# A hybrid decoder layer on one core: no written order of instructions, a timeline model that ranks them all, plain products for the first output pairs, and eight gate columns moved from w_out to the query projections

## The chip, the cores and the metric

The kernel runs on one core of a Trainium2 chip. A core has TensorE (PE; matrix products, with weight loads listed as PEld), VectorE (DVE), ScalarE (ACT), GpSimd (POOL) and SyncE (SP). Each engine works through its own queue of instructions in order and waits on semaphores for the others. Here SP's queue issues the loads of weights and inputs, POOL's queue issues the traffic with intermediate tensors in the chip's memory.

The metric is the device time of one execution, in microseconds (us), given as a median over runs.

## The reference

One decoder layer for 512 tokens of width D = 2048, in fp32. Cut to what matters:

```python
mod = silu(c) @ w_ada + b_ada                       # 6 x 2048 numbers
sh1, sc1, g1, sh2, sc2, g2 = split(mod, 6)
h = modulate(rms_norm(x, norm1_g), sh1, sc1)        # h * (1 + sc1) + sh1
u = h @ w_in                                        # conv, q and 3 x (k, v) columns, gates
y_conv = B * causal_depthwise_conv3(C * H)          # 1024 channels
y_attn = nsa_attention(q, ...)                      # 8 heads: compressed, selected, window
x = x + g1 * (concat([rms_norm(y_conv), rms_norm(y_attn)]) @ w_out)
h = modulate(rms_norm(x, norm2_g), sh2, sc2)
x = x + g2 * (square(relu(h @ w_ff1)) @ w_ff2)      # 8192 hidden columns
out = rms_norm(x, normf_g)
```

## The kernel before

**Arithmetic.** The products need more accuracy than one pass gives. Each operand is split into a high half (a rounded copy, made by ScalarE) and a low half (the difference, made by VectorE). `mm3` (L93 to L95) issues three matmuls for each pair of 128 x 128 blocks: high x high (L93), high x low (L94) and low x high (L95). So each weight blob of 128 x 1024 costs one ScalarE pass (`wh`, L83 or L800) and one VectorE pass (`wl`, L84 or L801) before its matmuls. Activations lie with channels on the partitions and tokens along the row.

**adaLN.** Each of the 96 columns of `mod` is a dot product of 2048 numbers with silu(c): two VectorE multiply-and-sum passes over a 128 x 1024 load of w_ada (`scr`, L134, followed by a short read of the sum), and one small instruction (L139) that adds both halves and the bias.

**The front** (from L98). Sums of squares of x give the row norm `rs` (L178), spread over the partitions as a 128 x 512 tile and copied to `rb`. Then 32 steps follow, each with one 128 x 1024 blob of `w_kv` or `w_cv` and one k of the 16 channel blocks: 24 matmuls of 512 columns into eight banks. Beside them VectorE computes the scale and shift column of each next k, multiplies x by `rb` (`tokens`, L260) and makes the low half of h (`low`, L267); what is left of time goes to further w_ada columns from a list `todo`. All of this stage is written with `pinned[0] = True`: `pin` (L67 to L69) then marks an instruction to stay in program order, and the program interleaves the work by hand, with a count of VectorE time (`clock`) against the steps' (`ready`).

**After the front** `pinned[0]` is False (L411), and the tile framework's scheduler, in its default ranking, decides the order on each engine. The projections follow: the convolution columns (`project`, `w_conv`), the compression of keys and values (`compress`), the value columns, then the query columns (`w_q`). At places in these loops `more_ada` takes columns from `todo`: 16 columns of the first gate, 32 of the second scale and shift, and 8 of the second gate (M_G2). Attention runs over 2 groups and 4 blocks of 128 queries. Between the blocks stand eight products of the convolution half with `w_oc` (`out_conv`, its banks named `pw`), which serve as filler for TensorE; behind the last block the attention row norm, `row_bcast` (L178 to L182), the scaling `ya` (L766) and the splits `mixa` (L89, L90) make the operands of the attention half.

**w_out.** The attention half is multiplied by eight `w_oa` blobs; in this loop `ada` also computes the last eight columns of the second gate through `raw_blob`. Then `kept` splits eight blobs of `w_oa2`, `late_out(0)` makes the low half of the tokens (256) of the other 1024 output channels, `late_out(1)` the high half.

**The feed-forward part.** Each of 32 pairs of w_ff1 is a 2 x 2 block product done with 7 products rather than 8 (Winograd's form of Strassen's scheme). The weights of a pair are four blobs A11, A21, A22, A12; `operands` makes the seven weight operands, with four sums or differences of 128 x 1024 on VectorE (`sub`, L875) and seven splits (`hilo`, L800 and L801). The token operands B1, U6, T5, B2, T7, B3, T4 stay in memory; `low_tokens` and `high_tokens` make them from the normed rows. A product is 24 matmuls of 256 columns into a bank `pf`. `ff1` combines the products, applies relu and square, makes the seven operands of the next stage (`gt`, `gb`) and stores them through POOL. In the second stage, 8 rounds f load the seven token operands (`tk<-g`) and run w_ff2 in the same way. `ahead` puts products B1 and B2 of the first three pairs ahead while `high_tokens` is computed.

The start of the feed-forward part before:

```python
    late_out(0)
    low_tokens()
    late_out(1)
    ahead(0, B1)
    row_norm(bankf, sacc, D, r2, 2, 4)
    ahead(1, B1)
    high_tokens(0)
    ...
    high_tokens(3)
    for p in range(32):
        ff1(p)
```

Of the kernel before, what the change touches and what calls it, by code (L numbers as in the profile page):

```python
# [15 lines left out]
P = 128  # L16
# [24 lines left out]
def hybrid_layer(ctx: ExitStack, tc: tile.TileContext, a, out):  # L41
# [56 lines left out]
    pinned[0] = True  # L98
# [43 lines left out]
    def ada(n, blob=None):  # L142
        acc = small.tile([P, 2], F32, name="acc")
        for i in range(2):
            if blob is None:
                w = slot(name="wa")[:, :1024]
                nc.sync.dma_start(out=w, in_=a["w_ada"][2 * n + i])
# [20 lines left out]
    def row_norm(bank, square, width, dst, t0=0, t1=NQ):  # L168
        total = bank()
        for t in range(t0, t1):  # L170
            nc.tensor.matmul(total[:, t:t + 1], square[:, t * P:(t + 1) * P], ones[:, 0:1],
                             start=True, stop=True)
        row_bcast(bank, total[:, t0:t1], width, dst[:, t0 * P:t1 * P])

    def row_bcast(bank, total, width, dst):
# [5 lines left out]
        if dst is not None:  # L181
            nc.scalar.activation(dst, ps[:, :n * P], AF.Copy)  # L182
# [64 lines left out]
    for i in range(4):  # L247
# [7 lines left out]
        + [M_G2 * NK + k for k in range(8)]  # L255
# [188 lines left out]
    nc.sync.dma_start(out=cw2, in_=a["vec"][:, V_END:])  # L444

    def compress(which, src):
# [3 lines left out]
        for hf in range(2):  # L450
            t = slot(name="ct")
            nc.vector.memset(t[:, 1024:SLOT], 0.0)
            tv = t[:, :1024].rearrange("p (l g n) -> p l g n", g=NG, n=32)
            n = 32 - hf
            for g in range(NG):
                nc.vector.tensor_tensor(
                    out=tv[:, :, g, :n],
                    in0=src[g].rearrange("p (n l) -> p l n", l=16)[:, :, hf:],
                    in1=pe[:, hf * 16:hf * 16 + 16, None].to_broadcast([P, 16, n]), op=OP.add)
            if hf:  # L460
                nc.vector.memset(tv[:, :, :, 31:], 0.0)
            hi = slot(F32R, name="chi")
            lo = slot(F32R, name="clo")
            nc.scalar.activation(hi, t, AF.Copy)
            nc.vector.tensor_tensor(out=lo, in0=t, in1=hi.bitcast(F32), op=OP.subtract)
# [18 lines left out]
        nc.scalar.activation(hid, pc[:64, :256], AF.Copy)  # L484
        nc.vector.tensor_tensor(out=tt, in0=hid, in1=hid, op=OP.mult)
        nc.vector.tensor_scalar(tt, tt, 0.044715, 1.0, op0=OP.mult, op1=OP.add)
        nc.vector.tensor_tensor(out=tt, in0=tt, in1=hid, op=OP.mult)
        nc.scalar.activation(tt, tt, AF.Tanh, scale=math.sqrt(2.0 / math.pi))
        nc.vector.tensor_scalar(tt, tt, 1.0, 0.5, op0=OP.add, op1=OP.mult)
        nc.vector.tensor_tensor(out=hid, in0=hid, in1=tt, op=OP.mult)  # L490
        pt = bank()
        for i in range(2):
            nc.tensor.transpose(pt[:, i * 64:i * 64 + 64], hid[:, i * P:(i + 1) * P], ident[:64, :64])
        hidt = temp([P, 2, NG, 32], name="hidt")
        nc.scalar.activation(hidt.rearrange("p i g n -> p (i g n)"), pt[:, :P], AF.Copy)
        yield
        if which == 0:
            pk = bank()
            for i in range(2):
                nc.tensor.matmul(pk[:, :64], w2[i], hidt[:, i].rearrange("p g n -> p (g n)"),  # L500
                                 start=i == 0, stop=i == 1)
            for g in range(NG):
                split(kslc[g][:, :, :32], pk[:, g * 32:g * 32 + 32])
        else:
            pad = temp([P, 2, NG, P], name="hpad")
            nc.vector.memset(pad, 0.0)
            nc.vector.tensor_copy(pad[:, :, :, :32], hidt)
            for g in range(NG):
                pv = bank()
                for i in range(2):  # L510
                    nc.tensor.matmul(pv[:, :P], pad[:, i, g], w2[i], start=i == 0, stop=i == 1)
# [7 lines left out]
    for j in range(8):  # L519
# [13 lines left out]
        if 3 * j >= 8:  # L533
            nc.scalar.activation(z, got[0], AF.Copy)
            got[0] = z
        nc.vector.tensor_tensor(out=v, in0=got[1], in1=got[0], op=OP.mult)
        nc.scalar.activation(z, v, AF.Identity, scale=cw[2], bias=vec[:, V_CB + j:V_CB + j + 1])
        for t, d in ((1, 1), (0, 2)):
            nc.vector.scalar_tensor_tensor(out=z[:, d:], in0=v[:, :T - d], scalar=cw[t], in1=z[:, d:],
                                           op0=OP.mult, op1=OP.add)  # L540
        nc.vector.tensor_tensor(out=y, in0=got[2], in1=z, op=OP.mult)
        if j == 0:
            sacc = accum()
            nc.scalar.activation(sacc, y, AF.Square)
        else:
            sq = temp(name="sq")
            nc.scalar.activation(sq, y, AF.Square)
            nc.vector.tensor_tensor(out=sacc, in0=sacc, in1=sq, op=OP.add)
# [7 lines left out]
    for g in range(NG):  # L556
# [13 lines left out]
        for t in range(NQ):  # L570
            if t % 2 == 0:
                vp = pair(F32R, name="vv").rearrange("p h (t c) -> p h t c", t=2)
            vv[g, t] = vp[:, :, t % 2]
            nc.scalar.activation(vv[g, t][:, 0], pv[t][:, :256], AF.Copy)
            nc.vector.tensor_tensor(out=vv[g, t][:, 1], in0=pv[t][:, :256],
                                    in1=vv[g, t][:, 0].bitcast(F32), op=OP.subtract)
            gt = gates[:, t, g].rearrange("p r b -> p (r b)")
            nc.scalar.activation(gt, pv[t][:, 256:268], AF.Tanh, scale=0.5)
            nc.vector.tensor_scalar(gt, gt, 1.0, 0.5, op0=OP.add, op1=OP.mult)
# [9 lines left out]
    def mixed(j):  # L589
        y = ys[j // 2][:, j % 2]  # L590
        nc.vector.scalar_tensor_tensor(out=y, in0=y, scalar=vec[:, V_GC + j:V_GC + j + 1], in1=rc,
                                       op0=OP.mult, op1=OP.mult)
# [13 lines left out]
    for g in range(NG):  # L606
# [9 lines left out]
        for n in range(NR):  # L616
# [3 lines left out]
            nc.scalar.activation(raws[-1], pq[n], AF.Copy)  # L620
# [20 lines left out]
    def out_conv(m):  # L641
# [8 lines left out]
        nc.vector.scalar_tensor_tensor(out=x1[m // 2][:, m % 2], in0=ps, scalar=col(M_G1, m),  # L650
                                       in1=out_conv.x[:, (m % 2) * T:(m % 2 + 1) * T],
                                       op0=OP.mult, op1=OP.add)

    def attention(g, qb):
# [4 lines left out]
        nc.vector.memset(pcx[:, NR:], 0.0)  # L659
        pc = pcx[:, :NR]  # L660
        cm = cmask[:, qb]
        for b in (1, 2):
# [7 lines left out]
            for r in range(NR):  # L670
                q = qs[g * NR + r]
                s = pss.tile([P, T], F32, name="s")
                nc.tensor.matmul(s[:, :w], q[:, 0, qc], kt[:, 0, c0:c0 + w], start=True, stop=False)
# [579 lines left out]
```

## Time and profile before

| what | value |
|---|---|
| median of 3 runs | 2223.15 us (2222.85 to 2224.5) |
| profiled execution | 2224.19 us |
| its span, first to last instruction | 2222.4 us |
| mean granted TensorE clock | 0.981 |
| TensorE busy, matmuls | 2131.6 us (96%), 14942 |
| VectorE busy, instructions | 1918.1 us (86%), 2998 |
| ScalarE busy | 1008.2 us (45%) |
| DMA | 453.61 MB, mean 204 GB/s |

The page counts the time in which an engine had at least one instruction in flight. Matmuls are pipelined and their ends are modelled, so that the spans of neighbours overlap: one of 256 columns is listed with 282 ns, though 427 of them start in 50 us. Idle time of TensorE is thus read better from the number of matmuls in a stretch than from the busy share. In a table of stretches each row has the stretch, its length, then for PE, PEld, DVE, ACT and POOL the busy time with the number of instructions in brackets, then the clock that was granted to TensorE (1.00 is full), the busy share of the DMA engines and the rate in GB/s. In a row of a group, "x176 | 211.0, 1220 | 8.1 <-DMA" reads: 176 instructions, 211.0 us busy, 1220 ns each, 8.1 us of idle time of that engine just before them, ended by a DMA. In a row of waits, "6.1, 1, 6.1" is the total, the number of times and the longest. In a timeline the first two numbers are the start and the duration in us.

The execution in stages, by that trace: the front up to 225, the projections up to about 575, attention up to about 793, w_out's attention half and `late_out` up to about 890, ff1 up to about 1575, ff2 to the end.

### The profile page before, as it was taken

To read this page: it belongs to the slowest core of one execution; us is meant where nothing else is said; L and a number is where in the kernel's file an instruction comes from. 1 tells how busy PE (TensorE), PEld (TensorE's weight loads), DVE (VectorE), ACT (ScalarE), POOL (GpSimd) and SP (SyncE) were. 2 spreads that over 40 slices of the span, in tenths; PEclk is the share of its full clock that TensorE was granted. 3 is DMA by queue.
4 is the path that set the end of the run, shared out by engine and by line. 5 is a ranking of instruction groups with operands and counts; after the bars stand their busy time and mean duration, and the time that the engine had idled before them with its cause. 6 is when DMAs were issued, how large, how long until landed. Compare 5 with 4: busy or idle time off the path is not lost.

```text
span 2222.4 us, 37637 instructions
## 1 busy us (share of the span) xinstructions
PE 2131.6 (96%) x14942; PEld 1969.9 (89%) x14942; DVE 1918.1 (86%) x2998; ACT 1008.2 (45%) x1468; POOL 193.6 (9%) x366
## 2 busy tenths in 40 slices
PE   6999989999999999799999999999899999999997
PEld 4777778898777779799999999999899999999996
DVE  8889978877496687999999999999799999999996
ACT  4431333222354435665666556666333333333353
POOL 0000000000000001021111111113211011011000
PEclk7999999999999999899999999999999999999998
DMA  8985686954211165276665666658865466366442
GB/s 343 336 323 180 237 313 256 356 216 180 86 39 57 57 266 185 81 233 209 199 196 195 199 211 196 201 190 283 296 241 195 157 237 233 119 237 235 151 146 95
DMA packets 143984, 453.61 MB, mean 204 GB/s; under 512 B 15809, under 2 KB 20161, under 8 KB 143809
## 3 DMA queue, kind: packets, MB, share of 16 engines
q1 hardware_dynamic: 91104, 322.22, 40.4%
q0 software_dynamic: 51616, 127.95, 17.2%
q8 instruction: 117, 1.92, 0.3%
q10 hardware_dynamic: 1088, 1.05, 0.1%
q14 instruction: 59, 0.48, 0.1%
HBM read 383.00 MB, written 68.16 MB: 203 GB/s over the span
## 4 chain that ended last, share of the span: by engine, by line
PE 75%; DVE 13%; ACT 5%; DMA 4%; issue 2%; SPq 0%; DVEq 0%; ACTq 0%; POOL 0%; POOLq 0%
PE pf L95 18%; PE pf L93 18%; PE pf L94 18%; PE ps L94 5%; PE ps L95 5%; PE ps L93 5%; DVE scr L134 3%; DVE wl L84 2%; DMA tk<-g 1%; DVE hl L801 1%; ACT wh L83 1%; PE pw L94 1%; PE pw L95 1%; PE pw L93 1%; PE pt L719 1%
## 5 line engine op out<-in xcount | busy, mean ns | idle before, releaser
L93 PE MATMUL pf<-tk,hl 128*128 128x256 f32 x3576 | 1008.0, 282 | 12.3 <-DMA tk<-g 6.0
L95 PE MATMUL pf<-tk,hl 128*128 128x256 f32 x3576 | 1005.5, 282 | 12.2 <-DVE hl L801 12.2
L94 PE MATMUL pf<-tk,hl 128*128 128x256 f32 x3576 | 1006.7, 282 | 1.3 <-DVE tk L872 1.3
L93 PEld LDWEIGHTS pf<-tk,hl 128*128 128x128 f32 x3576 | 678.2, 190 | 15.3 <-ACT hl L800 8.0
L95 PEld LDWEIGHTS pf<-tk,hl 128*128 128x128 f32 x3576 | 676.7, 190 | 14.8 <-DVE hl L801 14.7
L94 PEld LDWEIGHTS pf<-tk,hl 128*128 128x128 f32 x3576 | 677.0, 189 | 1.7 <-DVE tk L872 1.6
L800 ACT ACTIVATE hl<-rw 128x1024 fp32r<-128x1024 f32 x264 | 278.8, 1056 | 303.6 <-PE pf L95 254.9
L801 DVE TENSOR_TENSOR hl<-rw,hl 128x1024 fp32r<-128x1024 f32 x264 | 321.9, 1219 | 25.6 <-ACT hl L800 25.2
L800 ACT ACTIVATE hl<-sg 128x1024 fp32r<-128x1024 f32 x189 | 200.3, 1061 | 267.7 <-PE pf L95 242.9
L801 DVE TENSOR_TENSOR hl<-sg,hl 128x1024 fp32r<-128x1024 f32 x189 | 230.5, 1221 | 41.7 <-ACT hl L800 41.3
L134 DVE SCALAR_TENSOR_TENSOR scr<-wa,cs 128x1024 bf16<-128x1024 f32 x176 | 211.0, 1220 | 8.1 <-DMA wa<-in_w_ada 8.0
L83 ACT ACTIVATE wh<-raw 128x1024 fp32r<-128x1024 f32 (+1 forms) x105 | 110.8, 1059 | 221.0 <-PE ps L94 105.1
L84 DVE TENSOR_TENSOR wl<-raw,wh 128x1024 fp32r<-128x1024 f32 (+1 forms) x105 | 128.6, 1225 | 56.6 <-ACT wh L83 54.2
L875 DVE TENSOR_TENSOR sg<-sg,rw 128x1024 f32<-128x1024 f32 x126 | 153.5, 1219 | 0.9
L95 PE MATMUL ps<-h_m,wl 128*128 128x512 f32 x360 | 142.8, 397 | 2.5 <-DVE wl L84 2.4
L93 PE MATMUL ps<-h_m,wh 128*128 128x512 f32 x360 | 142.6, 396 | 2.4 <-ACT wh L83 1.2
L94 PE MATMUL ps<-h_m,wh 128*128 128x512 f32 x360 | 141.8, 394 | 0.0
L1049 DVE SCALAR_TENSOR_TENSOR x<-pf,mod,x 128x256 f32<-128x256 f32 x256 | 119.7, 479 | 17.9 <-PE pf L95 14.9
L93 PE MATMUL ps<-h,wh 128*128 128x512 f32 x280 | 113.2, 404 | 13.1 <-ACT wh L83 9.1
L95 PE MATMUL ps<-h,wl 128*128 128x512 f32 x280 | 113.7, 406 | 2.4 <-DVE wl L84 2.4
L94 PE MATMUL ps<-h,wh 128*128 128x512 f32 x280 | 113.3, 405 | 0.0
L1015 POOL DMA_DIRECT2D g<-gt x192 | 101.0, 532 | 86.4 <-DVE gt L872 81.2
(325 smaller groups left out, 2974.1 us busy)
## 6 DMA issues: line engine op xcount, KB each, us to landing
rw<-in_w_f SPq DMA_DIRECT2D x262, 512.0 KB, 4.3
wa<-in_w_ada SPq DMA_DIRECT2D x176, 512.0 KB, 6.2
tk<-g POOLq DMA_DIRECT2D x114, 512.0 KB, 8.1
g<-gt POOLq DMA_DIRECT2D x192, 256.0 KB, 5.0
raw<-in_w_conv SPq DMA_DIRECT2D x32, 512.0 KB, 6.6
raw<-in_w_kv SPq DMA_DIRECT2D x16, 512.0 KB, 5.4
raw<-in_w_cv SPq DMA_DIRECT2D x16, 512.0 KB, 4.5
raw<-in_cmp_w SPq DMA_DIRECT2D x16, 512.0 KB, 5.4
```

What stands on the lines that cost most here:

```text
L83: pin(nc.scalar.activation(wh[:, :cols], raw[:, :cols], AF.Copy))
L84: pin(nc.vector.tensor_tensor(out=wl[:, :cols], in0=raw[:, :cols], in1=wh[:, :cols].bitcast(F32), op=OP.subtract))
L93: pin(nc.tensor.matmul(ps, lh, rh, start=start, stop=False, skip_group_check=more))
L94: pin(nc.tensor.matmul(ps, lh, rl, start=False, stop=False, skip_group_check=more))
L95: pin(nc.tensor.matmul(ps, ll, rh, start=False, stop=stop, skip_group_check=more))
L134: pin(nc.vector.scalar_tensor_tensor(out=scr, in0=w, scalar=1.0, in1=cs[i].rearrange("p a b -> p (a b)"), op0=OP.mult, op1=OP.mult, accum_ ...
L719: nc.tensor.transpose(pt[:, r * P:(r + 1) * P], probs[b, r][:, kb * P:(kb + 1) * P], ident)
L800: nc.scalar.activation(dst[0], src, AF.Copy)
L801: nc.vector.tensor_tensor(out=dst[1], in0=src, in1=dst[0].bitcast(F32), op=OP.subtract)
L875: nc.vector.tensor_tensor(out=dst, in0=x, in1=y, op=op)
L1015: nc.gpsimd.dma_start(out=gd[p // 4][idx[j]][p % 4 // 2][:, p % 2], in_=g[:, j])
L1049: nc.vector.scalar_tensor_tensor(out=xm, in0=src, scalar=gate, in1=xm, op0=OP.mult, op1=OP.add)
```

## The change

1. `pinned[0]` is False in the front too. `pin` is put around nearly every instruction of the kernel, but since it is never switched on, it marks nothing. The framework is asked to rank with its timeline model over the whole kernel.
2. `todo` holds all 16 columns of the second gate rather than 8, so that `more_ada` takes the other 8 (16 loads of 512 KB, 16 dots) in the projections, and the w_out loop has none.
3. The start of the feed-forward part is rewritten. The first NP = 3 pairs are computed with plain products, 8 for each pair: A11 B1 + A12 B2 and A21 B1 + A22 B2 for the low half of the tokens, and the same blobs with T5 and B3 for the high half; the snapshot of the low half's first product is added back in `outcome`. `plan` lists the 24 products, `makes` after which product each blob's split is made, and `stay` which products reuse a split. Norm, low tokens and high tokens become generators (`norm_steps`, `low_tokens`, `high_tokens`) that `fill` advances, by counts of cost, between products. T5 is computed with the opposite sign; for the remaining pairs the split of the sum s1 is made with a factor of −1 (`minus`).
4. `late_out` is cut into `late_product` and `late_residual`; two products of 256 tokens share a bank. The second store of the last pairs (`g12d`) uses the buffer `gb`.

The built program has 72 matmuls more (24 plain products in place of 21), 14 VectorE instructions of 128 x 1024 fewer, one activation-table load more and 11 rows of SP's queue fewer.

```diff
-    pinned[0] = True
+    pinned[0] = False
...
-        + [M_G2 * NK + k for k in range(8)]
+        + [M_G2 * NK + k for k in range(NK)]
...
-        ada(M_G2 * NK + 8 + k, raw_blob)
...
-    late_out(0)
-    low_tokens()
-    late_out(1)
-    ahead(0, B1)
...
-    for p in range(32):
+    NP = 3
+    plan = []
+    for p in range(NP):
+        for b, i, u in ((A11, B1, 0), (A21, B1, 1), (A12, B2, 0), (A22, B2, 1)):
+            plan.append((p, b, i, u, 0, i == B1))
+    for p, order in ((2, (A21, A12, A22, A11)), (0, (A21, A22, A11, A12)), (1, (A11, A21, A12, A22))):
+        begun = set()
+        for b in order:
+            u = int(b in (A21, A22))
+            plan.append((p, b, T5 if b in (A11, A21) else B3, u, 1, u not in begun))
+            begun.add(u)
+    makes = {0: (3,), 1: (4,), 2: (5,), 3: (6,), 5: (7,), 6: (8,), 7: (9,), 8: (10,), 9: (11,), 13: (15,),
+             14: (18,), 15: (19,), 16: (20,), 19: (21,), 20: (22,), 21: (23,)}
+    stay = {12: 9, 13: 10, 14: 11, 16: 1, 17: 3}
...
+    def fill():
+        while clock[1] < clock[0] - 0.3:
+            g = next((g for g in waiting if not blocked.get(g)), None)
+            if g is None:
+                return
+            waiting.remove(g)
+            try:
+                c = next(g)
...
+    def product(task, makes, later):
+        between()
+        task()
+        clock[1] = max(clock[1], clock[0])
+        clock[0] += 2.82
+        for f in makes:
+            f()
+            clock[1] += 1.15
+        for f, cost in later:
+            f()
+            clock[1] += cost
+        fill()
...
+    def outcome(p):
+        xy = ffp.tile([P, 1024], F32, name="rw", bufs=6)
...
+        for u in range(2):
+            pin(nc.scalar.activation(x[:, u], banks2[p, u][:, LO], AF.Relu))
+        pin(nc.scalar.activation(x, x, AF.Square))
+        for u in range(2):
+            sub(y[:, 1 - u], snaps[p, u], banks2[p, u][:, HI], OP.add)
...
+    def pair_product(n):
+        p, b, i, u, hf, first = plan[n]
+        if hf == 0 and first:
+            banks2[p, u] = bankf()
+        run(banks2[p, u], made[stay.get(n, n)], tok[i], first, True, c=halves[hf])
...
+    for n in range(len(plan)):
+        product(lambda: pair_product(n), [lambda m=m: make(m) for m in makes.get(n, ())], later)
...
+    pinned[0] = False
+    for p in range(NP, 32):
         ff1(p)
...
-    with tile.TileContext(nc) as tc:
+    with tile.TileContext(nc, schedule_with_timeline_sim=True) as tc:
```

More of the change, by code (lines that the diff above doesn't have):

```diff
@@ L939, in operands, with run @@
         yield hilo(hl_tile(), a22)
[L941 removed]
+    def run(ps, w, toks, first, last, base=0, n=8, c=LO):
         wh, wl = w
@@ new lines, in hybrid_layer, with chain @@
+    later = []
+    for i in range(8):
+        product(lambda: late_product(0, i), (), later)
+        later = [(lambda i=i: late_residual(0, i), 0.8)]
+    for f, _ in later:
+        f()
+    later = []
+    def chain():
+        yield from norm_steps(0)
+        yield from low_tokens()
+    waiting.append(chain())
+    for i in range(8):
+        n = {1: 0, 2: 2, 7: 1}.get(i)
+        product(lambda: late_product(1, i), () if n is None else (lambda: make(n),), later)
+        later = [(lambda i=i: late_residual(1, i), 0.8)]
@@ L1036, in hybrid_layer @@
+    for f, _ in later:
+        f()
+    while waiting:
+        clock[0] += 10.0
+        fill()
+    pinned[0] = False
+    for p in range(NP, 32):
         ff1(p)
     ngate = consts.tile([P, NK], F32, name="ngate")
-    nc.vector.tensor_scalar(ngate, mod[:, M_G2 * NK:], -1.0, None, op0=OP.mult)
+    pin(nc.vector.tensor_scalar(ngate, mod[:, M_G2 * NK:], -1.0, None, op0=OP.mult))
     sacc = accum()
```

520 lines of the change are left out of this document (313 added, 207 removed).

## The prediction, made before the changed kernel had run

> **What bounds the kernel now.** I read the page's shares and chain first.
>
> ```profile
> PE 2131.6 (96%) x14942; PEld 1969.9 (89%) x14942; DVE 1918.1 (86%) x2998; ACT 1008.2 (45%) x1468; POOL 193.6 (9%) x366
> PE 75%; DVE 13%; ACT 5%; DMA 4%; issue 2%; SPq 0%; DVEq 0%; ACTq 0%; POOL 0%; POOLq 0%
> ```
>
> TensorE carries three quarters of the chain, VectorE is second. A busy share of 96% hides stalls, since matmul spans overlap; so I count matmuls in stretches (columns: stretch, its length, then busy us and count of PE, PEld, DVE, ACT, POOL, then granted clock, DMA share, GB/s).
>
> ```profile
> 0.00:27.40 27.40, 11.81 (x26) 6.44 (x26) 19.95 (x36) 16.21 (x21) 0.20 (x4) 0.73 0.92 362
> 27.40:60.00 32.60, 28.41 (x97) 20.70 (x98) 30.09 (x55) 12.77 (x18) 0.00 (x0) 0.86 0.84 324
> 60.00:225.00 165.00, 159.47 (x673) 125.15 (x671) 148.76 (x252) 52.68 (x69) 0.00 (x0) 1.00 0.77 281
> 275.00:300.00 25.00, 17.12 (x76) 13.53 (x75) 20.89 (x36) 7.63 (x9) 0.00 (x0) 0.80 0.80 297
> 500.00:550.00 50.00, 50.00 (x217) 40.58 (x216) 35.52 (x54) 13.40 (x16) 0.00 (x0) 1.00 0.50 190
> 550.00:600.00 50.00, 47.56 (x213) 39.06 (x212) 21.91 (x37) 17.65 (x31) 0.00 (x0) 0.96 0.30 105
> 575.00:793.00 218.00, 209.62 (x1049) 166.51 (x1048) 151.75 (x368) 101.58 (x258) 0.00 (x0) 0.98 0.17 60
> 776.00:794.00 18.00, 17.68 (x75) 13.28 (x75) 12.55 (x20) 10.01 (x18) 0.00 (x0) 1.00 0.26 88
> 793.00:875.00 82.00, 77.35 (x457) 67.36 (x456) 64.15 (x102) 27.58 (x38) 5.66 (x9) 1.00 0.72 270
> 875.00:975.00 100.00, 85.10 (x619) 81.39 (x618) 94.50 (x168) 66.39 (x124) 9.96 (x18) 0.90 0.40 131
> 1000.00:1050.00 50.00, 50.00 (x427) 50.00 (x426) 46.65 (x63) 30.66 (x43) 10.54 (x21) 1.00 0.67 214
> 1550.00:1600.00 50.00, 41.60 (x329) 40.84 (x329) 38.18 (x53) 19.53 (x27) 12.84 (x24) 0.93 0.96 356
> ```
>
> Undisturbed, 217 matmuls of 512 columns fill 50 us (0.230 each), and 427 of 256 columns do (0.117 each). By that measure the long feed-forward part (1000 to 1050) loses nothing, and three places lose most: the start, where the first projection matmul comes at 27.4; 275 to 300; and 875 to 975, the start of the feed-forward part, where 619 matmuls need 619 x 0.117 = 72.5 us and take 100: 27.5 lost, with VectorE busy 94.5.
>
> **The front** (24 matmuls for each of 32 steps). The built order of the changed kernel's instructions shows what the ranking does: 14 of the multiplications of x by the row norm, the second weight split and two dots now stand ahead of the first low half h, three weight blobs are loaded ahead of the first w_ada blob, and one more activation-table load stands before the first rs. The prices:
>
> ```profile
> L134 DVE SCALAR_TENSOR_TENSOR scr<-wa,cs 128x1024 bf16<-128x1024 f32 x176 | 211.0, 1220 | 8.1 <-DMA wa<-in_w_ada 8.0
> L134 DVE DVE_READ_ACCUMULATOR scr<-wa,cs 128x1 f32 x176 | 14.5, 83 | 0.0
> L139 DVE SCALAR_TENSOR_TENSOR mod<-acc,vec 128x1 f32<-128x1 f32 x96 | 20.8, 216 | 2.2
> L260 DVE TENSOR_TENSOR x<-x,rb 128x512 f32<-128x512 f32 x15 | 10.3, 685 | 0.0
> L84 DVE TENSOR_TENSOR wl<-raw,wh 128x1024 fp32r<-128x1024 f32 x97 | 118.4, 1222 | 51.1 <-ACT wh L83 48.8 <-PE ps L95 1.1 <-PE pw L95 0.5
> L178 ACT ACT_TABLE_LOAD  x2: 1283/1283/1283, 455.8 to 781.9; - x2
> 27.40 0.69 DVE L267 TENSOR_TENSOR h<-tmod,h 128x512 fp32r<-128x512 f32 x1 [0.40 <-ACT h L263]
> 27.42 0.80 PE L93 MATMUL ps<-h,wh 128*128 128x512 f32 x1 [2.57 <-ACT h L263]
> ```
>
> 14 x 0.685 + 1.22 + 2 x (1.22 + 0.08) = 13.4 us enter ahead of the low half; a few small pieces leave, and adding all VectorE durations in the two orders up to it gives 12.5. Up to the fourth low half the work is again about 23.5 us in both, so step 4 starts near 60 + 12.5 = 72.5. Up to the sixteenth the sums agree within 1.3 us: VectorE has its debt back by then. TensorE's floor is 24 x 0.230 = 5.5 us a step; 28 steps take 154.6, where they take 165 now. The front therefore ends between 72.5 + 154.6 = 227.1 (+2) and, if nothing is caught up and the table load counts, +13.8. VectorE is 90% busy there (148.76 of 165), so I take about half of the catch-up: **+6** (+2 to +14).
>
> **The projections.** In 275 to 300 the groups of 256 columns are these, and the waits end so:
>
> ```profile
> L95 PE MATMUL ps<-swh,clo 128*66 128x256 f32 x9 | 2.5, 280 | 0.0
> L94 PE MATMUL ps<-swl,chi 128*66 128x256 f32 x8 | 2.3, 285 | 1.5 <-DVE swl L84 1.5
> L93 PE MATMUL ps<-swh,chi 128*66 128x256 f32 x8 | 2.2, 280 | 0.0
> PE ps L93 <- ACT wh L83: 6.1, 1, 6.1
> ACT wh L83 <- DMA raw<-in_w_conv: 7.3, 2, 4.7
> ```
>
> 25 x 0.117 + 51 x 0.230 = 14.7, so 10.3 of the 25 us are lost: a convolution blob landed late behind a bunch of w_ada loads in SP's queue. The new queue mixes them more evenly, but the ranking can bunch others, for a wait of half that size: −10.3 to +5. I take **−2**, near no change, as the new order promises no gain for sure. The eight gate columns come back here: 16 dots x 1.30 + 8 x 0.216 = 22.5 us of VectorE and 16 loads, most of them queued ahead of attention's first maximum. Cover: VectorE idles 28.1 us in 550 to 600 alone, and DMA is at 0.30. I price that at nothing; with the cover gone it is at most 22.5. What is queued behind them is nm, for which the whole softmax waits.
>
> **Attention's end.** Now:
>
> ```profile
> 778.27 0.60 ACT L733 ACTIVATE sq<-pv 128x512 f32<-128x512 f32 x1 [1.55 <-PE pv L95]
> 778.91 1.07 DVE L737 TENSOR_REDUCE sr<-sq 128x128 f32<-128x512 f32 x1 [1.45 <-ACT sq L733]
> 781.93 1.28 ACT L178 ACT_TABLE_LOAD   x1
> 783.22 0.30 ACT L178 ACTIVATE rs<-tot,eps 128x4 f32<-128x4 f32 x1
> 785.74 0.60 ACT L182 ACTIVATE rc<-pt 128x512 f32<-128x512 f32 x1 [2.21 <-PE pt L197]
> 787.15 0.64 ACT L89 ACTIVATE mixa<-ya 128x512 fp32r<-128x512 f32 x1 [0.82 <-DVE ya L766]
> ```
>
> From 778.27 to 787.79 this chain makes the first operand of w_out, 9.5 us, and TensorE is busy 17.68 of 18 us with w_out matmuls of the conv half (pw), held back as filler. In the new order none is left there: after the last pv stand two small matmuls and then pf. So up to 9.5 us are exposed. The filler isn't lost: it runs between earlier attention matmuls, where TensorE had nothing in flight for 218 − 209.62 = 8.4 us at least. Exposed 9.5, less 8.4: +1 at best by this row, +9.5 at worst, and below nothing if the gaps between matmuls hidden in the busy share are filled too (−5). An idle stretch also costs clock: 25 us at 0.80 lose 5.0 clock-us, of which 3.0 lie in the idle 6.1; 2.0 remain. I take **+3** (−5 to +11.5).
>
> The Trainium skill, "TensorE: Matmul & The Clock Gate", Part 1, says that TensorE drops to half rate after an idle window of some 3.4 us and needs about 3.4 us of work to come back. The granted clock of 0.80 after the idle 6.1 us agrees with such a drop; an estimate by that page, half of 3.4 = 1.7 us for a gap, would put the sum 0.3 us lower.
>
> **w_out.** Here 8 gate columns and their 16 loads leave.
>
> ```profile
> L134 DVE SCALAR_TENSOR_TENSOR scr<-rw,cs 128x1024 bf16<-128x1024 f32 x16 | 19.1, 1221 | 1.8 <-DMA rw<-in_w_ada 1.8
> L800 ACT ACTIVATE hl<-rw 128x1024 fp32r<-128x1024 f32 x264 | 278.8, 1056 | 303.6 <-PE pf L95 254.9 <-DMA rw<-in_w_oa 20.9 <-DVE rw L875 15.6
> ```
>
> VectorE loses 20.8 of its 64.15 us, and w_oa blobs (20.9 us of ACT's waits) no longer queue behind gate blobs. TensorE's idle is 82 − 77.35 = 4.65, so −4.65 to 0; **−3**.
>
> **The first feed-forward pairs.** Three pairs go from 7 Winograd products each to 8 plain ones: 3 x 24 = 72 more matmuls x 0.117 = +8.4 us on TensorE. VectorE loses the 12 weight sums and two splits:
>
> ```profile
> L875 DVE TENSOR_TENSOR sg<-sg,rw 128x1024 f32<-128x1024 f32 x126 | 153.5, 1219 | 0.9
> L801 DVE TENSOR_TENSOR hl<-rw,hl 128x1024 fp32r<-128x1024 f32 x264 | 321.9, 1219 | 25.6 <-ACT hl L800 25.2
> PE pf L95 <- DVE hl L801: 9.2, 6, 3.1
> ```
>
> 14 x 1.22 = 17 us. In 875 to 975 VectorE then needs 94.5 − 17 = 77.5 and TensorE 72.5 + 8.4 = 80.9: TensorE becomes the bound. At best 100 becomes 80.9 (−19); at worst the 27.5 of stalls stay and 8.4 come on top. In the new order, weight splits come a product or more ahead, and only the norm's two short chains and the first splits can still wait: I leave 7 us of stall, 27.5 − 8.4 − 7 = **−12** (−19 to +8). Token work for the later products slides behind; it meets 3.35 us of spare VectorE in each 50 (1000 to 1050). Late next would be hl of the fourth pair.
>
> **The rest.** The sign turned on one sum makes the same splits at the same widths: 0. The steady pairs have no idle TensorE, and the new order makes each hl before its product: 0. The change of stage at 1550 to 1600 loses (427 − 329) x 0.117 = 11.5 us now, on token reloads, through the same queues:
>
> ```profile
> PE pf L93 <- DMA tk<-g: 6.0, 2, 5.4
> ```
>
> It stays: 0 (±4). One buffer for gb delays only stores on POOL: 0.
>
> Sum: 6 − 2 + 3 − 3 − 12 = −8. The profiled execution took 2224.19 (span 2222.4, 1.8 around it); 2216.2 on its scale. The median of three runs is 2223.15, 1.0 below, so 2215.
>
> **Rivals.**
> Slower: the stall at 875 to 975 is one of order, not of VectorE's volume. The norm's chain and the tokens come when they come, and more products only add 8.4. For it: the named waits for hl come to only 9.2 of 27.5. Against: VectorE is 94.5% busy there. In place of −12 it gives +8: 2235. It decides from a remaining stall of 19 us on. Chance 0.26.
> No change: the front's 12.5 and 1.3 us are kept whole, as VectorE's 90% leaves too little to catch up: +14 for +6, 2223. For it: 60 to 225 runs at 5.9 us a step where 5.5 is the floor, so it catches up slowly even now. Against: the sums agree by the sixteenth low half. Chance 0.13.
> Little change: the filler used early brings nothing, and attention's end is exposed whole with its slow clock: +11.5 for +3, 2223.5. Against: the 8.4 idle us. Chance 0.07.
> Much faster: the even queue removes the late convolution blob whole (−10.3 for −2), and with it the front catches up (+2 for +6): 2203. For it: w_ada loads no longer stand in bunches. Against: at 0.80 the DMA engines have little to spare in 275 to 300. Chance 0.12.
> That the change doesn't alter the order is excluded by the order itself.
>
> **How the numbers follow.** My forecast has 0.42, with its own range 2205 to 2225. The range over the cases, 2196 to 2240, takes in the slower rival and the bounds of the FFN start; it leaves out about 2 in 10. Within 0.2% (2218.7 to 2227.6) is about what a measurement of this kernel can't tell from no change. Faster: 0.33 of mine, 0.11 of the much faster, 0.05 of the two middle ones: 0.49. Same: 0.07, 0.01, 0.07: 0.15. Slower: 0.26, 0.02, 0.08: 0.36.
>
> **What would show it.** First low half near 40, and the 28 later steps near 5.6 us; no bunch of waits for in_w_conv near 280; TensorE empty some 8 us between the last pv and the first pf; in the 100 us after late w_out, over 760 matmuls rather than 619, and VectorE under 90%. A front that ends after 240, waits of nm for dots, or half clock through the first three pairs would make it wrong.

## The result and the profile after

The changed kernel takes 2227.93 us (median of 13 runs, 2226.73 to 2232.61), the kernel before 2223.38 us beside it. The ratio is 1.0019, with a 95% interval of 1.0012 to 1.0027: slower by about 0.2%, where 2215, a gain of 8 us, was forecast. The profiled execution took 2228.90, with a span of 2227.1.

The page of the changed kernel, its shares and its chain by engine:

```profile
PE 2136.5 (96%) x15014; PEld 1989.3 (89%) x15014; DVE 1892.3 (85%) x2975; ACT 1012.7 (45%) x1470; POOL 194.3 (9%) x366
PE 81%; DVE 6%; ACT 2%; issue 1%; DMA 1%; POOL 0%; DVEq 0%; ACTq 0%
```

VectorE's share of the chain fell from 13% to 6% and DMA's from 4% to 1%, as the change meant to do, and yet the time did not fall. Neither line says why: a matmul at half clock counts in the chain as TensorE like any other. The stages do. I cut both traces at the same events, each the first or last matmul of a kind in TensorE's timeline:

| stage (us) | before | after | difference | forecast |
|---|---|---|---|---|
| front, start to the end of its 32 steps | 225.4 | 222.1 | −3.3 | +6 |
| projections, to the last of w_q | 356.2 | 350.4 | −5.8 | −2 |
| attention, last of w_q to first product of w_oa | 211.6 | 234.5 | **+22.9** | +3 |
| w_out with the late products | 96.9 | 97.1 | +0.2 | −3 |
| first four pairs of ff1 | 107.2 | 102.3 | −4.9 | −12 |
| other 28 pairs of ff1 | 554.2 | 557.6 | +3.4 | 0 |
| ff2 | 655.4 | 648.5 | −6.9 | 0 |
| end | 15.5 | 14.7 | −0.8 | 0 |

(The forecast put its −12 for the first pairs into the first three; the fourth is included here because its start is part of what went wrong. Differences sum to +4.8, the spans differ by 4.7.)

The stretches of the changed kernel that answer to those of the prediction (columns: stretch, its length, busy us and count of PE, PEld, DVE, ACT, POOL, then the granted clock, DMA share, GB/s):

```profile
30.30:65.30 35.00, 26.73 (x96) 20.36 (x97) 35.00 (x68) 10.53 (x16) 0.00 (x0) 0.86 0.87 335
65.30:222.00 156.70, 156.09 (x673) 126.18 (x673) 138.97 (x241) 53.39 (x67) 0.00 (x0) 1.00 0.75 284
275.00:300.00 25.00, 25.00 (x129) 20.94 (x128) 22.18 (x35) 9.96 (x10) 0.00 (x0) 1.00 0.95 351
600.00:700.00 100.00, 84.61 (x407) 67.75 (x406) 71.35 (x183) 43.43 (x120) 0.00 (x0) 0.88 0.11 37
793.00:807.00 14.00, 3.31 (x8) 1.14 (x7) 8.70 (x16) 8.49 (x16) 0.00 (x0) 0.68 0.00 0
904.00:1006.00 102.00, 92.73 (x751) 91.38 (x750) 84.37 (x147) 64.53 (x115) 12.35 (x23) 0.95 0.47 158
975.00:985.00 10.00, 1.94 (x10) 1.44 (x9) 6.00 (x11) 5.19 (x9) 4.23 (x8) 0.70 1.08 359
1550.00:1600.00 50.00, 50.00 (x424) 50.00 (x424) 45.47 (x65) 25.69 (x34) 13.96 (x26) 1.00 1.02 370
```

Three stalls of before are gone: 275 to 300 has 129 matmuls rather than 76, the change of stage near 1560 loses nothing, and the first plain pairs run almost full. Two stalls are new, 793 to 807 and 975 to 985, and 600 to 700 has 407 matmuls. For before that last stretch is

```profile
600.00:700.00 100.00, 95.80 (x490) 75.85 (x491) 79.05 (x207) 48.95 (x138) 0.00 (x0) 0.97 0.11 38
```

### The profile page after: what moved, and what is told of

The parts are those of the page before. It is cut to its first block, busy times and chain, and to the rows that moved or that the text cites. A ratio compares the mean times of both kernels' runs of the same rounds, so it can differ in the third digit from the quotient of the medians.

```text
span 2227.1 us, 37794 instructions
## 1 busy us (share of the span) xinstructions
PE 2136.5 (96%) x15014; PEld 1989.3 (89%) x15014; DVE 1892.3 (85%) x2975; ACT 1012.7 (45%) x1470; POOL 194.3 (9%) x366
## 4 chain that ended last, share of the span: by engine, by line
PE 81%; DVE 6%; ACT 2%; issue 1%; DMA 1%; POOL 0%; DVEq 0%; ACTq 0%
PE pf L93 20%; PE pf L95 20%; PE pf L94 19%; PE ps L95 5%; PE ps L94 5%; PE ps L93 5%; PE pw L93 1%; PE pw L94 1%; PE pw L95 1%; DVE hl L806 1%; PE pt L719 1%; DVE x L1243 1%; DVE scr L134 1%; PE pv L94 0%; DVE nm L677 0%
## 5 line engine op out<-in xcount | busy, mean ns | idle before, releaser
L93 PE MATMUL pf<-tk,hl 128*128 128x256 f32 x3568 | 998.3, 282 | 12.7 <-ACT hl L805 8.2
L94 PE MATMUL pf<-tk,hl 128*128 128x256 f32 x3568 | 996.6, 281 | 0.0
L95 PE MATMUL pf<-tk,hl 128*128 128x256 f32 x3568 | 979.4, 282 | 0.5 <-DVE hl L806 0.5
L93 PEld LDWEIGHTS pf<-tk,hl 128*128 128x128 f32 x3568 | 675.0, 189 | 13.7 <-ACT hl L805 8.6
L806 DVE TENSOR_TENSOR hl<-rw,hl 128x1024 fp32r<-128x1024 f32 x269 | 328.2, 1220 | 51.5 <-ACT hl L805 49.9
L805 ACT ACTIVATE hl<-sg 128x1024 fp32r<-128x1024 f32 x151 | 160.2, 1061 | 275.5 <-PE pf L95 258.3
L134 DVE SCALAR_TENSOR_TENSOR scr<-wa,cs 128x1024 bf16<-128x1024 f32 x192 | 228.0, 1219 | 5.2 <-DMA wa<-in_w_ada 5.0
L806 DVE TENSOR_TENSOR hl<-sg,hl 128x1024 fp32r<-128x1024 f32 x151 | 184.2, 1220 | 36.1 <-ACT hl L805 35.9
L883 DVE TENSOR_TENSOR sg<-sg,rw 128x1024 f32<-128x1024 f32 x120 | 146.1, 1217 | 0.2
L93 PE MATMUL ps<-h_m,wh 128*128 128x512 f32 x360 | 142.0, 395 | 0.0
L95 PE MATMUL ps<-h_m,wl 128*128 128x512 f32 x360 | 124.6, 395 | 0.6 <-DVE wl L84 0.6
L94 PE MATMUL ps<-h,wh 128*128 128x512 f32 x280 | 112.6, 402 | 8.2 <-DVE h L267 8.2
L93 PE MATMUL ps<-h,wh 128*128 128x512 f32 x280 | 107.2, 401 | 3.0 <-ACT h L263 3.0
L95 PE MATMUL ps<-h,wl 128*128 128x512 f32 x280 | 101.8, 401 | 1.6 <-DVE wl L84 1.6
```

The costliest lines, as they stand in the source:

```text
L93: pin(nc.tensor.matmul(ps, lh, rh, start=start, stop=False, skip_group_check=more))
L94: pin(nc.tensor.matmul(ps, lh, rl, start=False, stop=False, skip_group_check=more))
L95: pin(nc.tensor.matmul(ps, ll, rh, start=False, stop=stop, skip_group_check=more))
L134: pin(nc.vector.scalar_tensor_tensor(out=scr, in0=w, scalar=1.0, in1=cs[i].rearrange("p a b -> p (a b)"), op0=OP.mult, op1=OP.mult, accum_ ...
L805: pin(nc.scalar.activation(dst[0], src, AF.Copy))
L806: pin(nc.vector.tensor_tensor(out=dst[1], in0=src, in1=dst[0].bitcast(F32), op=OP.subtract))
```

## The experiments

My theory after the result (A): the timeline ranking itself costs the 23 us in attention and gives the gain at the change of stage. The rival (B): the moved gate columns, or something else in the new program, delay attention.

**default_rank.** The changed kernel, ranked as before:

```diff
-    with tile.TileContext(nc, schedule_with_timeline_sim=True) as tc:
+    with tile.TileContext(nc) as tc:
```

> The changed kernel with the framework's default ranking in place of the timeline model, nothing else undone. Theory A (the ranking made the loss in attention and the gain at the change from the first to the second feed-forward stage): from the first score to the first w_out product it takes about 200 us again instead of 223, the change of stage loses about 11 us again, and the whole comes to about 2215 (2205 to 2225). Theory B (the moved gate columns or the new program text made the loss in attention): attention stays at about 223 us and the time at 2228 or above.

Measured: 2202.16 us, 0.990 (0.9885 to 0.9915). Attention took 211.0 and ff2 654.7, as before, and the front ended at 213.8. Attention's middle is full again:

```profile
600.00:700.00 100.00, 95.94 (x513) 76.20 (x513) 82.62 (x219) 51.73 (x144) 0.00 (x0) 1.00 0.15 48
```

w_out took 93.0 (−3.9 for the −3 forecast), but the first four pairs of ff1 103.7, only 3.5 less than before where −12 was forecast. Theory A holds on both counts; B does not by itself delay attention, since the gate columns and the new program stay in this kernel. I had expected 2215: freeing the front of its written order is worth far more under the default ranking than under the timeline one (below).

**before_timeline.** The kernel before, with nothing but the ranking changed:

```diff
-    with tile.TileContext(nc) as tc:
+    with tile.TileContext(nc, schedule_with_timeline_sim=True) as tc:
```

> The kernel before with the timeline ranking, the front still in written order, nothing else changed. Theory A: attention with its end grows by some 20 us to about 222, the change of stage loses nothing, the first pairs keep their 27 us of stalls: about 2235 (2225 to 2245). Theory B: attention stays near 200 us, the time near 2223.

Measured: 2236.42 us, 1.0057 (1.004 to 1.0074). Attention 234.2 and ff2 645.1, against 211.6 and 655.4: the ranking alone makes both the loss of 22.6 and the gain of 10.3. Attention's middle is thinned out in this old program too:

```profile
600.00:700.00 100.00, 84.76 (x418) 68.04 (x417) 71.57 (x180) 44.71 (x121) 0.00 (x0) 0.89 0.12 37
```

The projections took 349.6, 6.6 less than before, and w_out 94.4, 2.5 less, both without the moved gates. The first four pairs got worse (116.7 against 107.2). This is theory A from the other side.

**filler_held.** The changed kernel, with the last two w_out products of the conv half queued behind the last sum of squares. (There are sixteen of these products: two are written ahead of the first block, twelve behind the blocks, and these two behind the row norm.)

```diff
...
-        pin(nc.tensor.matmul(st[:, 0:1], sr, ones[:, 0:1], start=True, stop=True))
+        held.append(nc.tensor.matmul(st[:, 0:1], sr, ones[:, 0:1], start=True, stop=True))
...
         if j % 4 == 0:
-            out_conv(m)
+            with tc.issue_after(held[-1].ins):
+                out_conv(m)
```

> The changed kernel with the last two w_out products of the conv half issued on TensorE only behind the last sum of squares of attention. If the lost filler is the cause of the exposed end (12.4 us of empty TensorE), those 12 us go, and some of it comes back as gaps between the last blocks: 2219 (2216 to 2224). If the filler was doing as much good where it stood, the time stays at 2228.

Measured: 2220.25 us, 0.9983 (0.9974 to 0.9993). The time is in the range I gave, but not for the reason: attention took 233.4, only 1.1 less. The end is filled again, and the loss is elsewhere:

```profile
600.00:700.00 100.00, 84.88 (x402) 68.44 (x403) 69.90 (x179) 42.40 (x116) 0.00 (x0) 0.86 0.10 34
786.00:804.00 18.00, 13.98 (x57) 10.02 (x55) 10.58 (x18) 10.18 (x18) 0.00 (x0) 1.00 0.00 1
```

The row has 57 matmuls in 18 us where that of the changed kernel had 8 in 14, but the stretch from the last attention matmul to w_oa is 16.7 us, against 13.3, and 600 to 700 is as empty as in the changed kernel. The rest of the 7.7 us (9.5 between the two profiled executions) came in stages that the edit does not touch: front and projections −2.4, w_out −2.7, the matmul rate of ff1 and ff2 −3.5. The first two came without any edit in a second run of the changed kernel (after_again, below: −2.2 and −2.8), so they are no gain of this one. So the missing filler, which the prediction made the whole of its term, was not the main thing.

**gates_back.** Eight gate columns in the w_out loop again:

```diff
-        + [M_G2 * NK + k for k in range(NK)]
+        + [M_G2 * NK + k for k in range(8)]
...
+        ada(M_G2 * NK + 8 + k, raw_blob)
```

> The changed kernel with eight gate columns in the w_out loop again. Theory A: they were hidden in the projections, and w_out's stage now has 20.8 us of VectorE work more beside 77 us of TensorE work: 0 to +4, 2228 to 2232. Theory B (their dots delay attention): attention 10 to 20 us shorter, 2210 to 2218.

Measured: 2221.98 us, 0.999 (0.9981 to 0.9999). Attention 233.8: the dots do not delay it under this ranking either, and B is out. Nor did the time rise. w_out took 94.4 us, and a second run of the changed kernel (below) 94.3, so that under this ranking the move is worth nothing in w_out; most of the rest of the difference, 4.2 us, is again the matmul rate.

**only_ffn_start** and **default_front_pinned** take the gain under the default ranking apart. Both have the default ranking and the front in written order (`pinned[0] = True`); the first also has the gate columns back in w_out.

> The changed kernel with the default ranking, the front in written order and the eight gate columns in the w_out loop: of the change only the rewritten start of the feed-forward part remains. By the stages measured with the default ranking (first product to the end of the fourth pair 103.7 us against 107.2) it is worth 3.5 us: 2220 (2217 to 2222). If its gain is the forecast one, 2212.

> The changed kernel with the default ranking and the front in written order; the gate columns stay moved. If the freed front made the gain of the default ranking, the last projection product comes near 581 us instead of 567 and the time is about 2216 (2213 to 2219). If the moved gates and the new start made it, it stays at 2202 to 2206.

Measured: 2219.24 us (0.9984, 0.9974 to 0.9993) and 2212.89 us (0.995, 0.9935 to 0.9965). Beside 2202.16 this gives each part its price under the default ranking: the new start about 4 us, moving the gates 6.3 us (2219.24 − 2212.89; w_out 97.1 against 92.8, so 4.3 of it is in that stage), freeing the front 10.7 us (2212.89 − 2202.16; its end at 224.4 against 213.8, the last projection product at 579.5 against 567.2). Under the timeline ranking the front ends at 225.1 in written order (before_timeline) and at 222.1 when free, so there it is worth 3. I had expected 2216 for the second and got 2213, for I had left out what the gates are worth in w_out.

**late_sums.** In the changed kernel's trace, from 583 to 794, TensorE waited longest for these (columns: total us, times, longest):

```profile
PE pt L739 <- DVE sr L737: 5.2, 3, 2.5
PE pv L94 <- DVE tt L90: 3.1, 8, 1.0
PE s L673 <- ACT q L284: 2.7, 1, 2.7
PE pt L719 <- DVE ssq L740: 2.0, 1, 2.0
```

For the same operand `sr` the kernel before waited eight times, never over 0.5 us:

```profile
PE pt L739 <- DVE sr L737: 2.3, 8, 0.5
```

L739 is a product of one column, the sum of squares for attention's row norm; nothing needs it until the end. In the timeline order it comes to the head of TensorE's queue before its operand `sr` is there. Here VectorE makes rope pieces (`rt`) and a maximum (`nm`) between the squares and `sr` (rows left out between these):

```profile
609.56 0.60 ACT L733 ACTIVATE sq<-pv 128x512 f32<-128x512 f32 x1
609.57 0.68 DVE L272 TENSOR_TENSOR rt<-qr,rot 128x512 f32<-128x512 f32 x1
611.84 0.53 DVE L677 TENSOR_REDUCE nm<-s 128x1 f32<-128x384 f32 x1
612.28 1.01 DVE L737 TENSOR_REDUCE sr<-sq 128x128 f32<-128x512 f32 x1
613.35 0.38 PE L739 MATMUL pt<-ones,sr 128*128 128x1 f32 x2 [2.46 <-DVE sr L737]
```

The edit does all eight sums together at the end:

```diff
+    srs = slot(name="srs")[:, :1024].rearrange("p (b t) -> p b t", b=8)
...
-        sr = attc.tile([P, P], F32, name="sr")
+        sr = srs[:, g * NQ + qb]
         pin(nc.vector.tensor_reduce(out=sr, ...))
-        st = pst.tile([P, T], F32, name="pt")
-        pin(nc.tensor.matmul(st[:, 0:1], sr, ones[:, 0:1], start=True, stop=True))
-        pin(nc.vector.tensor_copy(ssq[:, g, qb:qb + 1], st[:, 0:1]))
...
+    st = pst.tile([P, T], F32, name="pt")
+    for b in range(8):
+        pin(nc.tensor.matmul(st[:, b:b + 1], srs[:, b], ones[:, 0:1], start=True, stop=True))
+    pin(nc.vector.tensor_copy(ssq.rearrange("p g q -> p (g q)"), st[:, :8]))
```

> The changed kernel, timeline ranking, with the eight one-column sums of squares of attention done together behind its last block instead of one behind each block. If the timeline order loses its time in attention because these short products stand at the head of the queue of TensorE before their operand is there (gaps of 2.6, 1.1, 2.3 and 2.0 us), last projection product to first w_out product falls from 234 to about 226: 2220 (2217 to 2224). If they are only the last of several waits at each place, it stays above 231: 2226 to 2229.

Measured: 2208.42 us, 0.9929 (0.9914 to 0.9944). Attention fell from 234.5 to 220.5, by 14, where I had expected 8 from the named waits. In that kernel:

```profile
600.00:700.00 100.00, 89.36 (x463) 73.81 (x464) 81.29 (x214) 51.12 (x147) 0.00 (x0) 0.93 0.12 39
778.00:792.00 14.00, 3.57 (x10) 1.46 (x10) 8.37 (x15) 8.49 (x16) 0.00 (x0) 0.67 0.00 0
```

The middle has 56 matmuls more in 100 us, and the granted clock rose from 0.88 to 0.93. The end is as empty as it was. (Each sum also took one of the two banks of the transposes until L740 had read it, and the edit frees that bank too; the wait of 2.0 above is the one that names it. How much of the 14 us is the bank and how much the queue was not told apart.)

**sums_and_filler.** As late_sums, with the last two products of the conv half queued behind the last sum:

```diff
...
+        last_sum = pin(nc.tensor.matmul(st[:, b:b + 1], srs[:, b], ones[:, 0:1], start=True, stop=True))
...
         if j % 4 == 0:
-            out_conv(m)
+            with tc.issue_after(last_sum.ins):
+                out_conv(m)
```

> The changed kernel, timeline ranking, with the sums of squares behind the last block and the last two w_out products of the conv half issued behind them. If the one-column sums in the queue and the exposed end are the two whole causes in attention, last projection product to first w_out product falls from 220.5 to about 212, as with the default ranking (211): 2200 (2197 to 2203). If the filler's place still makes no difference, as in filler_held, it stays at 220 and the time at 2208.

Measured: 2197.79 us, 0.9887 (0.9872 to 0.9901). Attention 216.4: with the sums out of the way, the filler is worth 4 us where alone it was worth 1. Not the 212 I expected. Some 5 us of the loss against the default order are left: 2.0 are a wait ahead of the first w_oa product (788.86), taken up in the next section, and the rest is not named. The total fell as far as I expected all the same, because w_out (91.8) and the steady rate (117.8 ns) came out better as well.

**next_pair_early.** In default_rank one wait stood out behind the plain pairs, as in the changed kernel itself (7.6 there):

```profile
PE pf L93 <- ACT hl L805: 7.2, 1, 7.2
```

ScalarE does the relu, square and splits of the last plain pair before the first weight split of the fourth pair. The edit, on default_rank, writes the four loads, the two sums and the first split of the fourth pair ahead of that work:

```diff
+    def ff1_operands(p):
+        return operands([raw_blob(a["w_f1"][p, b]) for b in range(4)], True)
...
     for n in range(len(plan)):
...
+        if n == 21:
+            ops = ff1_operands(NP)
+            begun = [next(ops)]
...
-    for p in range(NP, 32):
+    ff1(NP, itertools.chain(begun, ops))
+    for p in range(NP + 1, 32):
         ff1(p)
```

> The changed kernel with the default ranking and the four loads, the two sums and the first split of the fourth pair written ahead of the last plain pair's outcome. If the 7.4 us of waiting before the fourth pair come from the outcome's ScalarE work standing ahead of that split, they go: 2195 (2193 to 2198). If the blobs themselves are late, it stays at 2202.

Measured: 2195.03 us, 0.9869 (0.9852 to 0.9885). The first four pairs take 96.7 rather than 103.7, and from 935 to 960, where the fourth pair starts, only this is left:

```profile
PE pf L96 <- DVE hl L807: 1.5, 1, 1.5
```

**three_repairs.** sums_and_filler with the edit of next_pair_early, under the timeline ranking.

> As sums_and_filler, and the first split of the fourth pair written ahead of the last plain pair's outcome. If causes add, 7 us less than sums_and_filler: about 2193, beside next_pair_early's 2195. If the timeline ranking puts the split where it likes, no less than sums_and_filler.

Measured: 2193.79 us, 0.9869 (0.9855 to 0.9884). The first four pairs fell from 101.8 to 97.9, so the timeline ranking follows the edit as well. It is level with next_pair_early; both beat the kernel before by 1.3%.

**after_again** and **repeated_sums** ask what a steady matmul costs. The first is the changed kernel once more, the second repeats three one-column products:

```diff
-        for t in range(2):
+        for t in (0, 1, 0, 1, 0) if hf else (0, 1):
```

> The changed kernel once more. In its first trace a matmul of 256 columns took 118.5 ns in the steady feed-forward stretches where the kernel before took 117.8, which is some 7 us over the stage. If that belongs to the program, it is 118.5 again and the time 2228; if it belongs to the execution, the figure falls anywhere between 117.6 and 118.6 and the time with it.

> The changed kernel with three one-column products of the second norm in the feed-forward start repeated (the same result; three matmuls and their weight loads more on TensorE, some 0.4 us, nothing else moved). In the changed kernel a steady matmul of 256 columns takes 118.5 ns, the same in two executions, with the slowest at the seventh of the eight blocks of a product (120.5). If that follows from where the instructions lie in TensorE's stream, the pattern over the blocks changes and the mean falls anywhere from 117.6 to 118.6, worth up to 8 us. If it follows from the addresses of the tiles, the pattern and the 118.5 stay and the time is 2226.

Measured: 2225.53 us (1.0013, 1.0003 to 1.0022) and 2228.5 us (1.0019, 1.0009 to 1.0028). The stretch 1100 to 1400 in before, after, after_again and repeated_sums, in that order:

```profile
1100.00:1400.00 300.00, 300.00 (x2549) 300.00 (x2548) 275.19 (x366) 185.17 (x259) 57.38 (x109) 1.00 0.63 200
```

```profile
1100.00:1400.00 300.00, 300.00 (x2534) 300.00 (x2533) 271.75 (x362) 184.83 (x256) 55.47 (x105) 1.00 0.65 200
```

```profile
1100.00:1400.00 300.00, 300.00 (x2533) 300.00 (x2532) 272.06 (x362) 185.24 (x259) 55.46 (x105) 1.00 0.66 199
```

```profile
1100.00:1400.00 300.00, 300.00 (x2534) 300.00 (x2533) 272.14 (x362) 184.31 (x256) 56.53 (x107) 1.00 0.66 199
```

300 us hold 2549 matmuls in before and 2533 or 2534 in the other three: 117.7 ns against 118.4, at full clock and without a gap. It belongs to the program, not to the execution; and by the last run not to the place of an instruction in TensorE's stream, as the pattern over the eight blocks of a product is the same to 0.1 ns behind three more products. The two sets of runs of the changed kernel, 2227.93 and 2225.53, also show that differences of 2 to 3 us between the runs above are not to be read.

## Why the prediction was wrong

**The direction.** A gain of 8 us was forecast, and the kernel became slower by 4.5. The step that turned the sign is attention.

**Attention: the step that failed.** The prediction priced only the end of attention, "up to 9.5 us exposed", and credited the filler with gaps "where TensorE had nothing in flight for 8.4 us at least": +3. It was +22.9. What failed is the assumption that filler used early fills gaps. The timeline order took the filler from the end and at the same time made new gaps in the middle (600 to 700: 407 matmuls for 490), where short products come to the head of an in-order queue and wait for VectorE. late_sums, which moves eight of them, took 14 of the 23 us back, sums_and_filler 18. I had read the order at attention's end only; the place of L739 behind each block could be read in it just as well, and its operand's lateness from `sr`'s row, quoted in the prediction itself (1.07 us behind a ScalarE pass). The "range −5 to +11.5" was too narrow by a factor of two, since it bounded what leaves the cover and not what a wrong order adds.

The exposed end itself was real, 13.3 us from the last pv to the first w_oa product with two short products between them (four matmuls in the trace), but the prediction's chain is only a part of it. That chain, to the first `mixa`, took 8.1 us after the last pv (794.07 to 802.20). Then TensorE stood still for 4.8 us more:

```profile
800.79 5.39 DVE L766 SCALAR_TENSOR_TENSOR ya<-ya,vec,rc 128x512 f32<-128x512 f32 x8 [2.86 <-ACT rc L182]
801.57 5.33 ACT L89 ACTIVATE mixa<-ya 128x512 fp32r<-128x512 f32 x8 [0.82 <-DVE ya L766]
806.09 1.41 DVE L650 SCALAR_TENSOR_TENSOR x<-pw,mod,raw 128x512 f32<-128x512 f32 x2
806.99 1.62 PE L93 MATMUL pf<-mixa,wh 128*128 128x512 f32 x3 [6.87 <-ACT mixa L89]
```

The last row names `mixa`, but the first of the eight was there at 802.20. What ends 0.15 us before the start, in this run and in filler_held, gates_back, late_sums and sums_and_filler, is VectorE's first `x<-pw` (806.84 here, 788.71 in sums_and_filler), which reads a finished bank of the conv half; the order puts it behind all eight `ya`. In default_rank it ends at 774.74, among them, and w_oa starts at 778.19 without a wait. No run moved it, so this is read from traces and not shown by an edit.

**The front.** The first low half came at 38.49, near the 40 forecast, and the 28 later steps took 156.7 / 28 = 5.60 us each, as forecast. Wrong was "step 4 starts near 72.5": it started at 65.4. These rows show it (changed kernel, timeline, and waits from 30 to 66):

```profile
38.49 0.69 DVE L267 TENSOR_TENSOR h<-tmod,h 128x512 fp32r<-128x512 f32 x1
PE ps L94 <- DVE h L267: 8.2, 4, 5.4
```

TensorE's new order does the eight high x high products of a step (L93) first; they need no low half. So it started at 30.4 and waited in all 8.2 us for low halves, and the shift of 11 us at the first low half was 5.5 at step 4. With the full catch-up, which I had halved, the front ends 3.3 early. default_rank, which is free too but puts thirteen multiplications of x fewer ahead of the first low half, has that half at 30.80, step 4 at 57.0 and the end at 213.8. So the timeline order does cost 8 us, but against the free default order, not against the written one.

**The projections.** −5.8 for −2: the bunch at 275 to 300 went (76 to 129 matmuls), which I had put into a rival with 0.12, and a new stall of some 4 us stands at 408 (a wait of 2.7 for `hpad`, and a clock of 0.93 over 25 us). My argument against that rival, that DMA at 0.80 has little to spare, did not hold: the row above has 0.95. The ranking makes this gain too, for before_timeline has it without the other parts (349.6, against 350.4 here). The 16 dots that moved here cost nothing that the runs can show: gates_back has the same projections and all but the same attention.

**w_out.** −3 forecast; under the default ranking the move is worth −4.3, so the mechanism and the size were right there. Under the timeline ranking the stage took 97.1 in the first trace and 94.3 in after_again, but gates_back and before_timeline show 94.4 with the gate columns in the loop, so the ranking hides them by itself.

**The first pairs.** The forecast took stalls from 27.5 to 7. In 904 to 1006, 751 matmuls x 0.117 = 87.9 of 102: some 14 us are left, and one place holds most of it, 975 to 985 with 10 matmuls. "Late next would be hl of the fourth pair" named the place; I gave it no price. next_pair_early measured it: 7.0 us. With it the four pairs take 10.5 less than before under the default ranking, and 9.3 less under the timeline ranking (97.9 in three_repairs), near my −12. The slower rival (a stall of order, not of volume) was right in kind for half of the remainder.

**The steady pairs and the change of stage.** Both stood at 0. The change of stage lost 11.5 before and nothing now; before_timeline shows that the ranking does it (ff2 −10.3): in the changed order POOL's loads of tokens and its last stores alternate from 1545 to 1583, and no wait of TensorE is left. Of this the steady rate took back 3.4 in ff1 and, by ff2's 648.5 against 645.1 in before_timeline, about as much in ff2.

**Clock.** The Trainium skill, "TensorE: Matmul & The Clock Gate", Part 1, has the clock halve after an idle window and return after a few microseconds of work. The rows of the two new stalls agree in kind, with 0.68 and 0.70. In 600 to 700 the clock is 0.88: 0.12 x 100 = 12 clock-us are gone, where the kernel before lost 3, although the longest single gap there is 2.7 us, and 5 came back in late_sums. So a stretch of many short gaps cost clock here too, and the prediction, which charged 2.0 clock-us for one idle stretch at the end, left that out.

Sum of the steps that were wrong: attention +19.9 over the forecast, first pairs +7.1, w_out +3.2, steady rate +6.8; front −9.3, projections −3.8, change of stage −10.3. The errors come to +37 and −23, and the end adds −0.8: the forecast −8 became +5. That 2227.93 lies inside the range over the cases, 2196 to 2240, is luck and no merit of the working: that range was drawn for stalls in the first pairs, while the loss came in attention, and the forecast's own range, 2205 to 2225, was missed.

## What to carry to other kernels

When a change hands the order to a ranking, read the new order for every short instruction at the head of an in-order queue that waits for another engine, not only for where filler went: here moving eight one-column products, with the bank that each one held, gave back 14 us. Price the parts of such a change one by one with the ranking held fixed; three of the four parts were gains (4, 6 and 11 us) under the default ranking and the fourth, the ranking, cost 23 to 26 (2202.16 to 2225.53 and 2227.93). And a stage in which everything is covered still has a next thing in line: name it, and give it a price from the work that stands ahead of it in its engine's queue.

## What the runs showed of the hardware that was not expected

Back-to-back matmuls of 256 columns at full clock do not take the same time in every program: 117.6 ns (default_rank, next_pair_early) to 118.5 ns (the changed kernel) in 1100 to 1500, the same in two executions of one program, and unchanged when three products were added ahead in the stream. Between the kernel before (117.8) and the changed one this is some 7 us over ff1 and ff2, more than the difference that this change made in all. What sets it is open; the places of the tiles in memory may differ between these programs and are one candidate that no run here tested.
